# Neighbourhood attention, two heads at a time, on alternating halves of the matmul array

## The chip, the core and the metric

The kernel runs on one core of a Trainium2 chip. TensorE (PE) multiplies a stationary operand of at most 128 rows by 128 columns, loaded by a separate instruction (PEld), with a moving one and writes PSUM, which has eight banks of 128 partitions by 512 float32. VectorE (DVE), ScalarE (ACT) and GpSimd (POOL) work beside it, SyncE (SP) issues most DMA transfers. Each engine works through its own queue in order. The metric is device time of one execution: 2326.95 us, median of 3 runs (2325.53 to 2333.34).

## What is computed

Two transformer blocks follow each other, on 512 positions and 1024 features, in float32. The first has differential attention, gated linear attention and a large expert layer; the second has a Fourier mix, a convolution, a neighbourhood attention and an MLP. The change lies in the neighbourhood attention of the second block. There 8 heads of 64 features look from each of 8 x 64 grid positions at 8 rows by 16 columns around them, and at 256 context positions:

```python
s_loc = jnp.einsum("brqhd,brkhd->bhrqk", qg, kg) * scale + bias[None]
s_ctx = jnp.einsum("brqhd,bchd->bhrqc", qg, k_ctx) * scale
p = jax.nn.softmax(jnp.concatenate([s_loc, s_ctx], axis=-1), axis=-1)
o = (jnp.einsum("bhrqk,brkhd->brqhd", p[..., :n_loc], vg)
     + jnp.einsum("bhrqc,bchd->brqhd", p[..., n_loc:], v_ctx))
```

The output goes, with those of the Fourier mix and the convolution, through the projection `w_out` and is added to the stream `h`.

## The kernel before

Positions are stored column by column of the grid, so a block `b` of 128 queries is 16 grid columns, and its keys are 256 neighbouring positions from `KSTART[b]` on, with the columns out of reach masked by the bias. With 4 blocks and 8 heads there are 32 items; item `i` is head `i // 4`, block `i % 4`. Features of two heads share a tile of 128 partitions: head `h` lies in partitions `64 * (h % 2)` on of `ql`, `kl` (local keys) and `ks` (context keys).

One item runs in three stages, which `pipe` sets against each other by 0, 2 and 3 items:
- `na_scores`: the bias is fetched; scores of 128 queries against 256 local and 256 context keys go into one PSUM bank. Each of the two products is three matmuls (`mm3`, L221 to L223), since operands are split into a high and a low part. DVE adds the bias to the local half and takes the negative row maximum, ACT takes the exponential with a row sum, DVE the reciprocal and the scaling.
- `na_turn`: four transposes through PE into another bank, copied to `npt` by ACT.
- `na_out`: four matmuls (float32, two records each in the trace) of 64 value columns with `npt`, into partitions 0 to 63 of a bank that four blocks of a head fill; behind the fourth, `split` writes the high part (ACT) and the low part (DVE) into the mix tiles.

A fourth entry, `aside`, advances the convolution (`conv`) and the Fourier mix (`fourier`) by one piece per item, in the order of the list `side`. All PSUM tiles of the stage are `psB`, eight of one bank each. The order of instructions on each engine is the scheduler's, which works from the order of the code and the tiles' readiness; what it made of it is shown below.

Ahead of the stage, the values are projected, DVE ends the convolution's taps and then scales `h1` eight times (L1588). Behind it comes `w_out`: for each of 8 output tiles `wsplit` fetches 128 x 1024 weights, ACT and POOL split them, and PE runs 24 matmuls into `pa` (lines L221 to L223 again). The first weights of the MLP are fetched and prepared by `prep` in the same place.

One other place matters below: `da_scores`, in the first block. Its heads have two parts of 64 features each, in partitions 0 to 63 and 64 to 127; for each 128 queries it issues two matmuls of the lower part, into one PSUM tile of two banks, and then two of the upper part, into another:

```python
for c in range(2):
    p = psA()
    for hf in range(2):
        cs = slice(64 * c, 64 * c + 64)
        PE.matmul(p[:, hf, :264], qz[cs, h, nt * 128:nt * 128 + 128], kr[cs, h, hf * 264:hf * 264 + 264], ...)   # L757
```

Of the kernel before, what the change touches and what calls it, by code (L numbers as in the profile page):

```python
# [8 lines left out]
F32 = mybir.dt.float32  # L9
# [5 lines left out]
AF = mybir.ActivationFunctionType  # L15
OP = mybir.AluOpType
AX = mybir.AxisListType
# [5 lines left out]
N = 512  # L23
# [165 lines left out]
def program(tc, a, dbg=None):  # L189
    dbg = dbg or {}  # L190
    nc = tc.nc
# [28 lines left out]
    def mm3(out, lhs, rhs, first, last):  # L220
        PE.matmul(out, lhs[0], rhs[0], start=first, stop=False)  # L221
        PE.matmul(out, lhs[0], rhs[1], start=False, stop=False)  # L222
        PE.matmul(out, lhs[1], rhs[0], start=False, stop=last)  # L223

    def pipe(n, *stages):

        for i in range(n + max(g for _, g in stages)):
            for f, g in stages:
                if 0 <= i - g < n:
                    f(i - g)  # L230

    def split(hi, lo, raw, eng=V):
        S.copy(hi, raw)  # L233
        eng.tensor_sub(lo, raw, hi.bitcast(F32))  # L234
# [38 lines left out]
    def psB():  # L273
        return ps.tile([128, 512], F32, name="psB", bufs=4)
# [1333 lines left out]
    with ExitStack() as es:  # L1608
# [68 lines left out]
                yield  # L1677


        st_ = {}  # L1680

        def na_scores(i):
            h, b = divmod(i, 4)
            k0 = KSTART[b] * 8
            bias = nbp.tile([128, 256], F32, name="bias", bufs=4)
            nc.sync.dma_start(bias, a['nab'][b, h])
            p = psB()
            o = 64 * (h % 2)
            q = [t[o:o + 64, h // 2, b * 128:b * 128 + 128] for t in ql]
            mm3(p[:, 0:256], q, [t[o:o + 64, h // 2, k0:k0 + 256] for t in kl], True, True)  # L1690
            mm3(p[:, 256:512], q, [t[o:o + 64, h // 2] for t in ks], True, True)
            V.tensor_add(p[:, 0:256], p[:, 0:256], bias)
            z = np_.tile([128, 2], F32, name="nz", bufs=5)
            V.reduce_max(z[:, 0:1], p, AX.X, negate=True)
            e = np_.tile([128, N], F32, name="ne", bufs=3)
            S.activation(e, p, AF.Exp, bias=z[:, 0:1], accum_out=z[:, 1:2])
            V.reciprocal(z[:, 1:2], z[:, 1:2])
            V.tensor_scalar(e, e, z[:, 1:2], None, op0=OP.mult)
            st_[i] = e

        def na_turn(i):
            e = st_.pop(i)
            p = psB()
            for k in range(4):
                PE.transpose(p[:, k * 128:k * 128 + 128], e[:, k * 128:k * 128 + 128], ident)
            pt = np_.tile([128, 4, 128], F32, name="npt", bufs=3)
            S.copy(pt, p.rearrange("p (a b) -> p a b", a=4))
            st_['t', i] = pt

        def na_out(i):  # L1710
            h, b = divmod(i, 4)
            k0 = KSTART[b] * 8
            pt = st_.pop(('t', i))
            if b == 0:
                st_['o'] = psB()
            po_ = st_['o']
            for k in range(4):
                vv = vl[:, k0 // 64 + 2 * k] if k < 2 else vc[:, k - 2]
                PE.matmul(po_[:64, b * 128:b * 128 + 128], vv[:, h * 64:h * 64 + 64], pt[:, k], start=k == 0, stop=k == 3)
            if b == 3:  # L1720
                o = (h % 2) * 64
                split(mix[0][o:o + 64, 4 + h // 2], mix[1][o:o + 64, 4 + h // 2], po_[:64])

        def aside(i):
            for g in side[i:i + 1]:
                next(g, None)

        cg, fg = conv(), fourier()
        side = [cg] * 3 + [fg, cg, fg, cg] + [fg, cg] * 3 + [fg] * 8
        pipe(32, (aside, 0), (na_scores, 0), (na_turn, 2), (na_out, 3))  # L1730

    if 'mix2' in dbg:
        with tc.tile_pool(name="dbgp", bufs=1, reuse_waits="tile") as dbp:
# [184 lines left out]
```

## Time and profile before

| | |
|---|---|
| median of 3 runs | 2326.95 us |
| profiled execution | 2328.06 us |
| its span | 2326.3 us |
| mean granted TensorE clock | 0.986 of full speed |
| PE busy | 2237.2 us, 96% |
| DVE busy | 1720.4 us, 74% |
| ACT busy | 1005.9 us, 43% |
| POOL busy | 620.7 us, 27% |

Shares are means over a program of many stages; the attention of the second block takes about a twentieth of the span, from about 1788 to 1903 us. An instruction's time in the trace includes its way through the engine: matmuls that follow each other overlap, so their cost is read from start to start, not from their durations. The granted clock is 1.00 at 2.4 GHz and 0.50 at 1.2 GHz; a window's value is a mean.

### The profile page before, as it was taken

The page shows a single profiled execution, that of the slowest core. Times are in us where ns is not written, and L with a number is a line of the kernel's source. Part 1 is how long each engine was busy: PE and PEld are TensorE (multiplying, and loading weights), DVE is VectorE, ACT ScalarE, POOL GpSimd, SP SyncE. Part 2 cuts the span into 40 slices and gives each one's busy share as a digit, 9 for nine tenths or more (in the row PEclk, how much of TensorE's full clock was granted, in tenths as well). Part 3 has the DMA queues.
Part 4 walks back from the last instruction along what each step waited for, and adds up shares of the span by engine and source line. Part 5 has one row for each costly group of instructions (what it writes and reads, how often), then busy time and mean ns, then how long its engine had stood idle before and what let it go on. Part 6 is the DMA issues. An engine that isn't in the chain of part 4 may idle for free.

```text
span 2326.3 us, 31023 instructions
## 1 busy us (share of the span) xinstructions
PE 2237.2 (96%) x11457; PEld 1884.1 (81%) x11457; DVE 1720.4 (74%) x3188; ACT 1005.9 (43%) x1439; POOL 620.7 (27%) x418
## 2 busy tenths in 40 slices
PE   7999898999999989999999999999998999999997
PEld 6777456898889978889999999999776777888885
DVE  8998776799999778877777887878669566433434
ACT  5337774433378833333333333333344644322322
POOL 2113212344320122223343444444362022000001
PEclk9999999999999999999999999999999999999998
DMA  7760014433266899999899999999322221422320
GB/s 249 253 234 10 1 61 145 172 124 118 85 238 261 301 371 337 335 335 319 309 332 323 313 327 318 322 325 316 130 91 73 73 75 64 126 92 82 118 82 37
DMA packets 158153, 458.02 MB, mean 197 GB/s; under 512 B 15249, under 2 KB 61969, under 8 KB 155697
## 3 DMA queue, kind: packets, MB, share of 16 engines
q1 hardware_dynamic: 120800, 319.57, 39.7%
q0 software_dynamic: 37200, 136.46, 16.9%
q8 instruction: 90, 1.47, 0.3%
q14 instruction: 63, 0.51, 0.1%
HBM read 419.80 MB, written 36.18 MB: 196 GB/s over the span
## 4 chain that ended last, share of the span: by engine, by line
PE 77%; DVE 14%; ACT 3%; DMA 3%; issue 2%; POOL 1%; DVEq 0%; SPq 0%; POOLq 0%; ACTq 0%
PE pu L221 8%; PE po L222 7%; PE po L221 7%; PE po L223 7%; PE pu L222 7%; PE pu L223 7%; DVE ac L1516 3%; PE pm L222 2%; PE pm L223 2%; PE pm L221 2%; PE pa L221 2%; PE pa L222 2%; PE pa L223 2%; PE pq L1187 2%; DVE aw L322 2%
## 5 line engine op out<-in xcount | busy, mean ns | idle before, releaser
L221 PE MATMUL pu<-hn,uhi 128*128 128x384 f32 x1024 | 356.9, 349 | 1.4 <-ACT uhi L233 1.4
L223 PE MATMUL pu<-hn,ulo 128*128 128x384 f32 x1024 | 347.3, 339 | 5.4 <-DVE ulo L234 3.6
L222 PE MATMUL pu<-hn,uhi 128*128 128x384 f32 x1024 | 347.4, 339 | 0.0
L221 PE MATMUL po<-vhi,ch 128*128 128x512 f32 x768 | 301.1, 392 | 2.5 <-ACT ch L1308 2.5
L222 PE MATMUL po<-vlo,ch 128*128 128x512 f32 x768 | 301.2, 392 | 0.3 <-DVE vlo L1309 0.3
L223 PE MATMUL po<-vhi,cl 128*128 128x512 f32 x768 | 299.0, 390 | 0.0
L1200 POOL DMA_INDIRECT gr<-in_u,idx x128 | 144.9, 1132 | 445.9 <-DVE aact L1205 414.6
L233 ACT CAST whi<-wraw 128x1024 fp32r<-128x1024 f32 x104 | 108.8, 1049 | 321.2 <-PE pm L222 128.7
L1297 ACT CAST vhi<-vraw 128x1024 fp32r<-128x1024 f32 x128 | 134.8, 1053 | 250.7 <-PE po L223 129.0
L234 POOL TENSOR_TENSOR wlo<-wraw,whi 128x1024 fp32r<-128x1024 f32 x52 | 130.8, 2521 | 382.7 <-ACT whi L233 329.2
L233 ACT CAST uhi<-uraw 128x1024 fp32r<-128x1024 f32 x105 | 110.1, 1048 | 268.9 <-PE pu L222 241.3
L1200 POOL DMA_INDIRECT gr<-in_v,idx x128 | 156.7, 1224 | 226.7 <-DVE acc L1214 189.1
L223 PEld LDWEIGHTS pu<-hn,ulo 128*128 128x128 f32 x1024 | 192.6, 188 | 6.4 <-DVE ulo L234 3.9
L221 PEld LDWEIGHTS pu<-hn,uhi 128*128 128x128 f32 x1024 | 193.0, 188 | 5.4 <-ACT uhi L233 1.9
L222 PEld LDWEIGHTS pu<-hn,uhi 128*128 128x128 f32 x1024 | 193.2, 189 | 3.5
L1309 DVE TENSOR_TENSOR vlo<-vraw,vhi 128x1024 fp32r<-128x1024 f32 x128 | 156.3, 1221 | 47.4 <-ACT vhi L1297 47.4
L234 DVE TENSOR_TENSOR wlo<-wraw,whi 128x1024 fp32r<-128x1024 f32 x52 | 63.5, 1222 | 157.6 <-ACT whi L233 157.4
L223 PEld LDWEIGHTS po<-vhi,cl 128*128 128x128 f32 x768 | 144.6, 188 | 31.7 <-DVE cl L1310 0.3
L221 PEld LDWEIGHTS po<-vhi,ch 128*128 128x128 f32 x768 | 144.6, 188 | 31.3 <-ACT ch L1308 2.9
L222 PEld LDWEIGHTS po<-vlo,ch 128*128 128x128 f32 x768 | 144.4, 188 | 27.9 <-DVE vlo L1309 0.7
L1214 DVE SCALAR_TENSOR_TENSOR acc<-gr,aact,acc 128x1024 f32<-128x1024 f32 x126 | 154.4, 1277 | 0.0
L1205 DVE CUSTOM_DVE_ANT_0 gr<-gr,hnat 128x1024 f32<-128x1024 f32 x128 | 152.5, 1218 | 0.0
(584 smaller groups left out, 5066.8 us busy)
## 6 DMA issues: line engine op xcount, KB each, us to landing
uraw<-in_ut SPq DMA_DIRECT2D x129, 512.0 KB, 4.9
vraw<-in_v SPq DMA_DIRECT2D x128, 512.0 KB, 5.5
aw<-in_ada SPq DMA_DIRECT2D x48, 512.0 KB, 5.0
gt<-gd SPq DMA_DIRECT2D x42, 480.0 KB, 7.4
wraw<-in_m SPq DMA_DIRECT2D x32, 512.0 KB, 3.7
xraw<-in_m SPq DMA_DIRECT2D x32, 512.0 KB, 4.3
gd<-gs SPq DMA_DIRECT2D x6, 2048.0 KB, 10.1
sd<-ge SPq DMA_DIRECT2D x56, 192.0 KB, 2.3
```

The costliest lines, as they stand in the source:

```text
L221: PE.matmul(out, lhs[0], rhs[0], start=first, stop=False)
L222: PE.matmul(out, lhs[0], rhs[1], start=False, stop=False)
L223: PE.matmul(out, lhs[1], rhs[0], start=False, stop=last)
L233: S.copy(hi, raw)
L234: eng.tensor_sub(lo, raw, hi.bitcast(F32))
L322: V.tensor_tensor_reduce(out=t, in0=w, in1=sil[:, q], scale=1.0, scalar=0.0, op0=OP.mult, op1=OP.add, accum_out=o)
L1200: G.indirect_dma_start(r, None, src, bass.IndirectOffsetOnAxis(ap=idx[:, j:j + 1], axis=0))
L1205: V.tensor_tensor_reduce(out=r, in0=r, in1=hnat, scale=1.0, scalar=0.0, op0=OP.mult, op1=OP.add, accum_out=aact[:, j:j + 1])
L1214: V.scalar_tensor_tensor(A, r, aact[:, j:j + 1], A, op0=OP.mult, op1=OP.add)
L1297: S.copy(wh, raw)
L1309: V.tensor_sub(wl, raw, wh.bitcast(F32))
L1516: V.scalar_tensor_tensor(ac[:, t], cv[:, t, j:j + N], w, ac[:, t], op0=OP.mult, op1=OP.add)
```

## The change

The 32 items become 16, each a pair of heads (`hp`) and a block. `na_scores` takes two banks and issues the same matmul for the head in partitions 0 to 63 and for the one in 64 to 127 in turn; `na_turn` transposes both heads; `na_out` alternates between output partitions 0 to 63 and 64 to 127 of one bank, and one `split` of 128 partitions follows four blocks. The small tiles move into a pool of their own (`nae`), with 6 buffers for the exponentials (three pairs) and 4 for the transposed ones (two pairs). The list `side` is shorter, and `aside` now stands behind the scores.

```diff
@@ -1677,57 +1677,68 @@
                 yield
 
 
+
         st_ = {}
+        nep = es.enter_context(tc.tile_pool(name="nae", bufs=1, reuse_waits="tile"))
+        HALVES = (slice(0, 64), slice(64, 128))
 
         def na_scores(i):
-            h, b = divmod(i, 4)
+            hp, b = divmod(i, 4)
             k0 = KSTART[b] * 8
-            bias = nbp.tile([128, 256], F32, name="bias", bufs=4)
-            nc.sync.dma_start(bias, a['nab'][b, h])
-            p = psB()
-            o = 64 * (h % 2)
-            q = [t[o:o + 64, h // 2, b * 128:b * 128 + 128] for t in ql]
-            mm3(p[:, 0:256], q, [t[o:o + 64, h // 2, k0:k0 + 256] for t in kl], True, True)
-            mm3(p[:, 256:512], q, [t[o:o + 64, h // 2] for t in ks], True, True)
-            V.tensor_add(p[:, 0:256], p[:, 0:256], bias)
-            z = np_.tile([128, 2], F32, name="nz", bufs=5)
-            V.reduce_max(z[:, 0:1], p, AX.X, negate=True)
-            e = np_.tile([128, N], F32, name="ne", bufs=3)
-            S.activation(e, p, AF.Exp, bias=z[:, 0:1], accum_out=z[:, 1:2])
-            V.reciprocal(z[:, 1:2], z[:, 1:2])
-            V.tensor_scalar(e, e, z[:, 1:2], None, op0=OP.mult)
-            st_[i] = e
+            bias, pp, es_ = [], [psB(), psB()], []
+            for h in range(2):
+                bias.append(nbp.tile([128, 256], F32, name="bias", bufs=4))
+                nc.sync.dma_start(bias[h], a['nab'][b, 2 * hp + h])
+            for keys, at, sl in ((kl, 0, slice(k0, k0 + 256)), (ks, 256, slice(0, 256))):
+                for t, (x, y) in enumerate(((0, 0), (0, 1), (1, 0))):
+                    for p, o in zip(pp, HALVES):
+                        PE.matmul(p[:, at:at + 256], ql[x][o, hp, b * 128:b * 128 + 128], keys[y][o, hp, sl], start=t == 0,
+                                  stop=t == 2)
+            for p, bt in zip(pp, bias):
+                V.tensor_add(p[:, 0:256], p[:, 0:256], bt)
+                z = nep.tile([128, 2], F32, name="nz", bufs=6)
+                V.reduce_max(z[:, 0:1], p, AX.X, negate=True)
+                e = nep.tile([128, N], F32, name="ne", bufs=6)
+                S.activation(e, p, AF.Exp, bias=z[:, 0:1], accum_out=z[:, 1:2])
+                es_.append((e, z))
+            for e, z in es_:
+                V.reciprocal(z[:, 1:2], z[:, 1:2])
+                V.tensor_scalar(e, e, z[:, 1:2], None, op0=OP.mult)
+            st_[i] = es_
 
         def na_turn(i):
-            e = st_.pop(i)
-            p = psB()
-            for k in range(4):
-                PE.transpose(p[:, k * 128:k * 128 + 128], e[:, k * 128:k * 128 + 128], ident)
-            pt = np_.tile([128, 4, 128], F32, name="npt", bufs=3)
-            S.copy(pt, p.rearrange("p (a b) -> p a b", a=4))
-            st_['t', i] = pt
+            pts = []
+            for e, _ in st_.pop(i):
+                p = psB()
+                for k in range(4):
+                    PE.transpose(p[:, k * 128:k * 128 + 128], e[:, k * 128:k * 128 + 128], ident)
+                pt = nep.tile([128, 4, 128], F32, name="npt", bufs=4)
+                S.copy(pt, p.rearrange("p (a b) -> p a b", a=4))
+                pts.append(pt)
+            st_['t', i] = pts
 
         def na_out(i):
-            h, b = divmod(i, 4)
+            hp, b = divmod(i, 4)
             k0 = KSTART[b] * 8
-            pt = st_.pop(('t', i))
+            pts = st_.pop(('t', i))
             if b == 0:
                 st_['o'] = psB()
             po_ = st_['o']
             for k in range(4):
                 vv = vl[:, k0 // 64 + 2 * k] if k < 2 else vc[:, k - 2]
-                PE.matmul(po_[:64, b * 128:b * 128 + 128], vv[:, h * 64:h * 64 + 64], pt[:, k], start=k == 0, stop=k == 3)
+                for h, o in enumerate(HALVES):
+                    PE.matmul(po_[o, b * 128:b * 128 + 128], vv[:, (2 * hp + h) * 64:(2 * hp + h) * 64 + 64], pts[h][:, k],
+                              start=k == 0, stop=k == 3)
             if b == 3:
-                o = (h % 2) * 64
-                split(mix[0][o:o + 64, 4 + h // 2], mix[1][o:o + 64, 4 + h // 2], po_[:64])
+                split(mix[0][:, 4 + hp], mix[1][:, 4 + hp], po_)
 
         def aside(i):
             for g in side[i:i + 1]:
                 next(g, None)
 
         cg, fg = conv(), fourier()
-        side = [cg] * 3 + [fg, cg, fg, cg] + [fg, cg] * 3 + [fg] * 8
-        pipe(32, (aside, 0), (na_scores, 0), (na_turn, 2), (na_out, 3))
+        side = [cg, fg, cg, fg, cg, fg, cg, fg, cg, fg, cg] + [fg] * 5
+        pipe(16, (na_scores, 0), (aside, 0), (na_turn, 2), (na_out, 3))
 
     if 'mix2' in dbg:
         with tc.tile_pool(name="dbgp", bufs=1, reuse_waits="tile") as dbp:
```

How it moves instructions. On PE, in the late part of the attention, one item stood like this before (`kl0`, `kl1` are the high and low parts of the local keys, `ks` of the context keys, `ql` of the queries; tiles of one name differ by their number):

```order
L221 MATMUL psB_17139<-kl0_15410,ql0_15408 128x256
L222 MATMUL psB_17139<-kl1_15411,ql0_15408 128x256
L223 MATMUL psB_17139<-kl0_15410,ql1_15409 128x256
L221 MATMUL psB_17139<-ks0_15412,ql0_15408 128x256
L222 MATMUL psB_17139<-ks1_15413,ql0_15408 128x256
L223 MATMUL psB_17139<-ks0_15412,ql1_15409 128x256
L1705 MATMUL psB_17153<-ident_58,ne_17092 128x128 x4
L1719 MATMUL psB_17132<-npt_17130,vl_15414 64x128 x2
L1719 MATMUL psB_17132<-npt_17130,vc_15420 64x128 x2
```

Now the two banks of a pair alternate, and so do the two heads' `npt` in the outputs (the last four of the scores, the transposes and the first half of the outputs):

```order
L1695 MATMUL psB_17158<-ks1_15413,ql0_15408 128x256
L1695 MATMUL psB_17159<-ks1_15413,ql0_15408 128x256
L1695 MATMUL psB_17158<-ks0_15412,ql1_15409 128x256
L1695 MATMUL psB_17159<-ks0_15412,ql1_15409 128x256
L1714 MATMUL psB_17190<-ident_58,ne_17069 128x128 x4
L1714 MATMUL psB_17197<-ident_58,ne_17074 128x128 x4
L1730 MATMUL psB_17204<-npt_17139,vl_15414 64x128
L1730 MATMUL psB_17204<-npt_17146,vl_15414 64x128
L1730 MATMUL psB_17204<-npt_17139,vl_15414 64x128
L1730 MATMUL psB_17204<-npt_17146,vl_15414 64x128
```

So between two changes from scores to transposes there stand twelve score matmuls where there were six, eight transposes and eight output matmuls.

On DVE, in the same part, the reciprocal and scaling of an item (L1697, L1698) stood among the bias addition and maximum (L1692, L1694) of the next:

```order
L1692 TENSOR_TENSOR psB_16806<-psB_16806,bias_16804 128x256
L1698 TENSOR_SCALAR ne_16788<-ne_16788,nz_16786 128x512
L1694 TENSOR_REDUCE nz_16814<-psB_16806 128x1
L1692 TENSOR_TENSOR psB_16833<-psB_16833,bias_16831 128x256
L1697 RECIPROCAL nz_16814<-nz_16814 128x1
L1694 TENSOR_REDUCE nz_16841<-psB_16833 128x1
L1698 TENSOR_SCALAR ne_16816<-ne_16816,nz_16814 128x512
L1697 RECIPROCAL nz_16841<-nz_16841 128x1
```

Now, in most pairs, addition (L1698), maximum (L1700), reciprocal (L1705) and scaling (L1706) of the same two heads follow each other:

```order
L1698 TENSOR_TENSOR psB_16812<-psB_16812,bias_16814 128x256
L1698 TENSOR_TENSOR psB_16813<-psB_16813,bias_16816 128x256
L1700 TENSOR_REDUCE nz_16831<-psB_16812 128x1
L1700 TENSOR_REDUCE nz_16836<-psB_16813 128x1
L1705 RECIPROCAL nz_16831<-nz_16831 128x1
L1706 TENSOR_SCALAR ne_16833<-ne_16833,nz_16831 128x512
L1705 RECIPROCAL nz_16836<-nz_16836 128x1
L1706 TENSOR_SCALAR ne_16838<-ne_16838,nz_16836 128x512
L234 TENSOR_TENSOR mx1_16285<-psB_16844,mx0_16284 128x512
```

The reciprocal waits for ACT's exponential of its own head. Work of another item no longer stands between a pair's maxima and its reciprocals; in a few pairs, three of them near the end, the next pair's additions stand between its two reciprocals.

At the start of the stage, PE had the convolution's mean (L1623), one item's scores, and the convolution's second product (L1633):

```order
L1598 MATMUL psB<-ident,sg 128x128 x8
L1623 MATMUL psB<-ac,ones 128x512 x2
L221 MATMUL psB<-kl_15410,ql_15408 128x256
L222 MATMUL psB<-kl_15411,ql_15408 128x256
L223 MATMUL psB<-kl_15410,ql_15409 128x256
L221 MATMUL psB<-ks_15412,ql_15408 128x256
L222 MATMUL psB<-ks_15413,ql_15408 128x256
L223 MATMUL psB<-ks_15412,ql_15409 128x256
L1633 MATMUL psB<-csq,ones 128x512 x2
```

Now a pair's scores stand ahead of the mean, and behind it come the second pair's and the Fourier mix's first products:

```order
L1623 MATMUL psB<-ac,ones 128x512 x2
L1695 MATMUL psB<-kl_15410,ql_15408 128x256 x2
L1695 MATMUL psB<-kl_15411,ql_15408 128x256 x2
L1695 MATMUL psB<-kl_15410,ql_15409 128x256 x2
L1695 MATMUL psB<-ks_15412,ql_15408 128x256 x2
L1695 MATMUL psB<-ks_15413,ql_15408 128x256 x2
L1695 MATMUL psB<-ks_15412,ql_15409 128x256 x2
L1657 MATMUL psB<-dft,ul 128x256 x8
```

The third pair's scores follow, and only then the convolution's second product.

## Rows read from the trace of the kernel before

**Rows 1.** the page, part 1: engine, busy us, share of the span, instructions

```profile
span 2326.3 us, 31023 instructions
PE 2237.2 (96%) x11457; PEld 1884.1 (81%) x11457; DVE 1720.4 (74%) x3188; ACT 1005.9 (43%) x1439; POOL 620.7 (27%) x418
```

**Rows 2.** the timeline, the stage's ends: start us, us, engine, line, operation, tiles, shapes, count

```profile
1788.27 5.39 DVE L1588 SCALAR_TENSOR_TENSOR h<-h,cols,rsy 128x512 f32<-128x512 f32 x8
...
1893.81 13.43 SPq L1756 DMA_DIRECT2D wraw<-in_m  x3
...
1897.56 2.13 DVE L1698 TENSOR_SCALAR ne<-ne,nz 128x512 f32<-128x512 f32 x1
...
1902.65 0.79 PE L221 MATMUL pa<-mx,whi 128*128 128x512 f32 x1
```

**Rows 3.** busy windows: length, PE, PEld, DVE, ACT, POOL (instructions), PEclk, DMA share, GB/s

```profile
1790.00:1795.00 5.00, 0.93 (x7) 0.73 (x7) 5.00 (x9) 0.71 (x2) 0.00 (x0) 1.00 0.03 11
1795.00:1800.00 5.00, 5.00 (x16) 2.80 (x16) 1.32 (x3) 4.48 (x6) 0.00 (x0) 0.66 0.11 26
...
1870.00:1880.00 10.00, 10.00 (x74) 8.11 (x73) 6.95 (x18) 5.85 (x13) 0.00 (x0) 1.00 0.20 55
```

**Rows 4.** the timeline, PE, one head in the late part of the attention

```profile
1870.22 0.38 PE L221 MATMUL psB<-kl,ql 64*128 64x256 f32 x1
...
1871.13 0.66 PE L1705 MATMUL psB<-ident,ne 128*128 128x128 f32 x4
1871.71 0.65 PE L1719 MATMUL psB<-npt,vl 128*64 128x128 f32 x4
...
1872.73 0.39 PE L221 MATMUL psB<-kl,ql 64*128 64x256 f32 x1
```

**Rows 5.** the timeline, scores of the first block's attention: both halves, one half, weight loads

```profile
193.84 1.17 PE L757 MATMUL psA<-kr,qz 64*128 64x264 f32 x8
...
272.84 1.15 PE L757 MATMUL psA<-kr,qz 64*128 64x264 f32 x4
...
193.84 0.20 PEld L757 LDWEIGHTS psA<-kr,qz 64*128 64x128 f32 x2
```

**Rows 6.** the timeline, DVE and ACT, the softmax of one head

```profile
1825.68 0.43 DVE L1692 TENSOR_TENSOR psB<-psB,bias 128x256 f32<-128x256 f32 x1 [2.73 <-PE psB L223]
...
1826.15 0.69 DVE L1694 TENSOR_REDUCE nz<-psB 128x1 f32<-128x512 f32 x1
...
1826.87 0.69 ACT L1696 ACTIVATE ne<-psB,nz 128x512 f32<-128x512 f32 x1
...
1827.68 0.16 DVE L1697 RECIPROCAL nz<-nz 128x1 f32<-128x1 f32 x1 [0.84 <-ACT ne L1696]
...
1827.88 0.49 DVE L1698 TENSOR_SCALAR ne<-ne,nz 128x512 f32<-128x512 f32 x1
```

**Rows 7.** the timeline, DVE and ACT, instructions that follow each other at once

```profile
1800.70 0.41 DVE L1692 TENSOR_TENSOR psB<-psB,bias 128x256 f32<-128x256 f32 x1
...
1801.02 0.47 DVE L1698 TENSOR_SCALAR ne<-ne,nz 128x512 f32<-128x512 f32 x1
1801.41 0.68 DVE L1694 TENSOR_REDUCE nz<-psB 128x1 f32<-128x512 f32 x1
...
1802.08 0.69 ACT L1696 ACTIVATE ne<-psB,nz 128x512 f32<-128x512 f32 x1
...
1802.76 0.68 ACT L1696 ACTIVATE ne<-psB,nz 128x512 f32<-128x512 f32 x1
```

**Rows 8.** instruction groups by line, 1790 to 1905: busy us, mean ns, idle before

```profile
L1707 ACT COPY npt<-psB 128x512 f32<-128x512 f32 x32 | 18.7, 585 | 23.1 <-PE psB L1705 23.0
...
L234 DVE TENSOR_TENSOR mx<-psB,mx 64x512 fp32r<-64x512 f32 (+1 forms) x10 | 6.8, 682 | 6.7 <-ACT mx L233 6.7
...
L1639 ACT ACT_TABLE_LOAD x2 | 2.6, 1283 | 0.0
```

**Rows 9.** busy windows, in the first block's attention, columns as in rows 3

```profile
235.00:240.00 5.00, 3.74 (x20) 2.68 (x19) 3.62 (x7) 5.00 (x14) 1.26 (x2) 1.00 0.00 0
```

## Prediction

> **What bounds the kernel now.** I read the page's part 1, then the busy windows around the attention, then the timeline of one head there, and last the rows of DVE and ACT between. The program is bound by TensorE: PE is busy for 96% of a span of 2326.3 us [rows 1], so time saved on another engine pays only where PE waits. The stage that changes begins where DVE ends the rescaling of `h1`, at 1788.27 + 5.39 = 1793.66, and ends with the first matmul of the output projection at 1902.65 [rows 2]: 109.0 us, 4.7% of the span. Two things fill it. From about 1805 on PE never rests: in 1870 to 1880 it is busy for all 10 us, DVE for 6.95, ACT for 5.85 [rows 3]. At the start PE is busy for 0.93 us of 5, a hole of 4.07, and then runs 5 us at a mean granted clock of 0.66 (1.2 GHz for most of it) [rows 3].
>
> One head and block costs PE 1872.73 - 1870.22 = 2.51 us in the late, undisturbed part: scores 0.91, four transposes 0.58, eight output matmul records 1.02 (a float32 matmul leaves two records) [rows 4]. 32 of them are 80.3 us. So the side work on PE (convolution and Fourier products) with all other waits is at most 109.0 - 80.3 - 4.1 = 24.6.
>
> **Removed and added on PE: scores.** A head's scores use 64 of the array's 128 rows, and the kernel before gives all of a head's matmuls the same half. Whether two halves run beside each other is shown in the first block's attention, whose scores have 64 rows as well: with one half alone four records take 1.15 us; with four on the lower half, then four on the upper, eight take 1.17, and two weight loads begin within the same 0.20 us [rows 5]. So eight cost what four cost, and I price twelve score matmuls of a pair like six: 0.91 us instead of 1.82.
>
> **Outputs.** They alternate between column halves, which this trace nowhere does: 16 records of a pair take between 1.02 (full overlap) and 2.04 (none). I take 1.02, since the nearest rows, those on row halves, show full overlap of matmuls and of loads.
> The Trainium skill, "TensorE: Matmul & The Clock Gate", Measured speedup vs the span model, gives 2.38 times for three column tiles; an estimate from it is 1.6 for two, so 1.28 us, and the sum below would stay, since PE isn't its bound. No run so far shows it.
>
> **Transposes** stay at eight per pair, 1.16. PE's step is then 0.91 + 1.16 + 1.02 = 3.09 us per pair against 5.02; 16 steps and the side work are 49.4 + 24.6 = 74.0, or 16 x 4.11 + 24.6 = 90.4 if column halves queue. None of DVE's and ACT's work on the scores goes away, so they are late next.
>
> **DVE and ACT.** In the new order DVE does a step as add, add, reduce, reduce, and then the reciprocals and scalings of the same two heads, which wait for both exponentials on ACT. The chain of one pair, by rows of single heads: first add 0.32 (to the next instruction), second add to its reduce 0.47, reduce to exponential 0.72, first to second exponential 0.68, exponential to reciprocal 0.81, reciprocal to scaling 0.20, scaling to the next instruction 0.39 [rows 6, 7]. Sum 3.59 us per pair, 57.4 for 16. Its bound from below is DVE's work alone: the 6.95 us busy in 1870 to 1880 hold one subtraction of 0.68 and 10/2.51 heads, so 1.57 a head, 3.15 a pair, 50.4 for 16 [rows 3, 8]. A few steps of the new order do mix pairs, so the truth lies between; I take 57.4, since most steps stand in series.
>
> What comes on top:
> - ACT's table loads. Per step ACT has 3.59 less two exponentials (0.68) and two copies (0.585), so 1.06 us free. Three times a side function needs two loads of 1.28 and an activation as long as an exponential, 0.69, 3.3 each [rows 6, 8]: 3 x (3.3 - 1.06) = 6.7. The first exponential's load adds 1.28. Together 8.0. ACT's other side work, 18 copies and casts of 0.59 and two weight casts of about twice that (twice the columns), is 13.0 and fits into the 17.0 free in 16 steps.
> - DVE's side work: 15 instructions like the subtraction of 0.68 and four like the add of 0.43, 11.9 us [rows 6, 8]. DVE stands still 3.59 - 3.15 = 0.44 a step, 7.0 in all; the order is fixed, so I let half of it take side work: 8.4.
> - The end: from the last scaling's end, 1897.56 + 2.13 = 1899.69, to 1902.65 were 2.96 us [rows 2]; a pair has four more transposes, 0.58: 3.5.
> - Waits that no row shows, for PSUM banks above all: eight banks; two pairs of scores, one pair of transposes and one output tile take seven, a side product the eighth. Lower end nothing; upper end the scores of the next pair in series with DVE each time, 0.91 x 16 = 14.6. I take 3, near the lower end, because seven fit.
>
> Sum: 57.4 + 8.0 + 8.4 + 3.5 + 3 = 80.3 us from 1793.66, against 109.0: 28.7 gained. PE needs 74.0 and may start before: two pairs' scores and sixteen Fourier records now stand ahead of the convolution's second product, where the hole of 4.07 was.
>
> **What moves along.** The biases are the same 32 transfers; two are freed per step and four buffered. The weights of the projection are split by ACT two steps before the end. SP issues the first MLP load at 1893.81, when the last scores are done, 8.8 us before the projection [rows 2]; now that distance is about 3.6 + 3.5 = 7.1, so POOL's work on it may come up to 2 us late for PE; I put it at 0 and keep 2 for the range. Everything behind is as long as before and moves forward as a block.
>
> The profiled execution took 2328.06 us, 1.1 above the median of the three timed (2326.95). 2328.1 - 28.7 = 2299.4, less 1.1: **2298 us**.
>
> **Rivals.**
> 1. *Column halves queue.* PE bounds: from about 1788.3, 90.4 + 3.5 end at 1882.2, 20.5 earlier than 1902.65: 2306. For it: no row shows columns side by side. Against: rows of the array do.
> 2. *Hand-offs.* The next pair's scores wait for banks that ACT hasn't emptied; the upper end of the waits, 14.6 for 3: a gain of 17, 2310, and some us more where a Fourier step takes two banks. The Trainium skill, "TensorEngine Tiling (Array Packing)", PSUM Bottleneck, warns of this: tiling speeds up TensorE but not the emptying of PSUM. The trace agrees as far as DVE and ACT are already busy for 70% and 59% of 1870 to 1880 [rows 3].
> 3. *The halves don't overlap at all* (the change doesn't do what it says): 80.3 + 24.6 from 1788.3, plus 3.5, ends at 1896.7; only the hole goes, 6 us: 2321. Against it stand the rows of the first attention [rows 5].
> 4. *Slower: the clock falls.* PE, now waiting for DVE in each step, is granted 1.2 GHz through the stage, and its 74.0 us become 148: the end at 1788.3 + 148 + 3.5 = 1939.8 is 37 later, 2364. It decides once PE is the bound at that clock, that is when over half the stage runs so (74.0 + half of 74.0 passes 109). For it: after the hole of 4.07 us the mean was 0.66. Against: in 235 to 240 PE is busy for 3.74 of 5 us and the clock stays 1.00 [rows 9], and a step with 3.09 of some 4.5 us busy is more like that.
>
> **How the numbers follow.** The forecast has 0.61, its own range 2288 to 2306 (DVE's bound from below takes 7 off, hand-offs and the late MLP load put up to 8 on). Rival 1 has 0.17, rival 2 0.13, rival 3 0.05, rival 4 0.04. The range 2286 to 2314 leaves out rivals 3 and 4, a third of rival 2 and the forecast's faster tail, under 0.2. A difference under 0.3%, 7 us, is about what a measurement of this kernel can't tell from none; rival 3 is within it. So faster 0.91, same 0.05, slower 0.04.
>
> **What would show it.** In the profile after: score matmuls in pairs, twelve in about 0.9 us; sixteen output records in about 1.0 (1.3 still fits, 2.0 is rival 1); steps of 3.5 to 4.5 us with DVE waiting for ACT's exponentials and PE idle for about a us in each; clock 1.00; the first projection matmul about 80 us behind the rescaling's end. A step over 4.6 us with DVE waiting for PE's scores would be rival 2, a mean clock under 0.8 over the stage rival 4. The forecast is wrong if the first projection matmul comes less than 15 us earlier than before.

## The result, and the profile after

The changed kernel takes **2298.09 us** (median of 4 runs, 2296.13 to 2300.76), the kernel before 2328.18 us (median of 4, 2325.53 to 2333.34): a ratio of 0.9866, 95% interval 0.9853 to 0.9879. The profiled execution took 2299.26 us.

The page of the changed kernel, its span and part 1, against [rows 1]:

```profile
span 2297.4 us, 31031 instructions
...
PE 2208.4 (96%) x11457; PEld 1862.9 (81%) x11457; DVE 1715.4 (75%) x3184; ACT 999.7 (44%) x1435; POOL 622.6 (27%) x418
```

The timeline of the changed kernel at the stage's ends, against [rows 2]:

```profile
1791.79 5.39 DVE L1588 SCALAR_TENSOR_TENSOR h<-h,cols,rsy 128x512 f32<-128x512 f32 x8
...
1860.26 17.26 SPq L1767 DMA_DIRECT2D wraw<-in_m  x3
...
1873.04 0.64 PE L221 MATMUL pa<-mx,whi 128*128 128x512 f32 x1
```

The stage runs from 1791.79 + 5.39 = 1797.18 to 1873.04: 75.9 us against 109.0, so 33.1 less. The spans differ by only 28.9, because the stage began 3.5 us later in this execution, and what follows it took 424.4 us against 423.7. The code ahead is the same; over the profiled kernels of this case DVE's L1588 starts anywhere from 1784.4 to 1794.2, so those 3.5 us are within the spread between executions.

The busy windows over the stage, first of the kernel before, then of the changed one (length, PE, PEld, DVE, ACT, POOL with their instructions, PEclk, DMA share, GB/s):

```profile
1793.66:1902.65 108.99, 103.59 (x630) 76.92 (x631) 66.04 (x150) 67.03 (x129) 6.78 (x3) 0.96 0.23 68
```

```profile
1797.18:1873.04 75.86, 68.98 (x606) 51.47 (x604) 61.04 (x146) 60.68 (x125) 6.78 (x3) 0.96 0.32 98
...
1810.00:1820.00 10.00, 7.95 (x60) 6.84 (x60) 8.96 (x20) 9.66 (x15) 0.00 (x0) 0.83 0.24 72
...
1830.00:1840.00 10.00, 10.00 (x83) 6.86 (x84) 8.68 (x23) 7.06 (x17) 0.00 (x0) 1.00 0.14 42
1840.00:1850.00 10.00, 10.00 (x92) 7.04 (x94) 8.32 (x20) 8.00 (x18) 0.00 (x0) 1.00 0.27 72
1850.00:1860.00 10.00, 10.00 (x128) 8.40 (x124) 8.58 (x21) 9.30 (x22) 4.88 (x2) 1.00 0.82 270
1860.00:1873.00 13.00, 9.55 (x92) 7.46 (x88) 8.22 (x19) 6.88 (x16) 1.90 (x1) 0.88 0.36 123
```

PE is busy for 34.6 us less in this window and stands still for 6.9 us instead of 5.4: 34.6 - 1.5 = 33.1. The window's start hides a shift. While DVE runs L1588, just ahead of it, PE was busy for half of the time before and is busy for all of it now:

```profile
1788.27:1793.66 5.39, 2.64 (x11) 1.19 (x9) 5.39 (x9) 0.59 (x1) 0.00 (x0) 1.00 0.34 129
```

```profile
1791.79:1797.18 5.39, 5.39 (x37) 3.70 (x37) 5.39 (x9) 0.59 (x1) 0.00 (x0) 1.00 0.34 129
```

With that stretch counted in, PE is busy for 74.4 us instead of 106.2, 31.9 less, and stands still for 6.9 instead of 8.2.

DVE and ACT are busy for 80% of the stage now, where it was 61%. In the middle, from 1812.12 to 1860.79, PE still never waits. One step there, the timeline of PE, against the head in [rows 4]:

```profile
1850.36 0.62 PE L1695 MATMUL psB<-kl,ql 64*128 64x256 f32 x6
1850.82 0.52 PE L1695 MATMUL psB<-ks,ql 64*128 64x256 f32 x6
1851.27 1.09 PE L1714 MATMUL psB<-ident,ne 128*128 128x128 f32 x8
1852.29 0.66 PE L1730 MATMUL psB<-npt,vl 128*64 128x128 f32 x8
1852.78 0.61 PE L1730 MATMUL psB<-npt,vc 128*64 128x128 f32 x8
1853.32 0.62 PE L1695 MATMUL psB<-kl,ql 64*128 64x256 f32 x6
```

Twelve scores take 0.91 us, as six did; sixteen output records 1.03, as eight did (1.02); eight transposes 1.02 instead of twice 0.58. A pair costs 2.96 us instead of 5.02. Over 16 pairs that is 14.6 from the rows, 16.2 from the columns and 2.2 from the transposes: 33.0, against the 31.9 by which PE's busy time fell. The overlap accounts for the gain to about 1 us.

PE's waits in the stage sum to 6.9 us. They stand at both ends; four of the seven, in order of time:

```profile
1800.29 0.62 PE L1695 MATMUL psB<-kl,ql 64*128 64x256 f32 x5 [0.80 <-DVE ac L1625]
...
1812.12 1.01 PE L1695 MATMUL psB<-kl,ql 64*128 64x256 f32 x5 [2.05 <-DVE crb L252]
...
1864.37 0.63 PE L1714 MATMUL psB<-ident,ne 128*128 128x128 f32 x4 [0.49 <-DVE ne L1706]
...
1868.38 0.63 PE L1714 MATMUL psB<-ident,ne 128*128 128x128 f32 x4 [2.14 <-DVE nz L1705]
```

The second is a wait for a PSUM bank: the scores take the bank that DVE's L252 reads last for the convolution. The last two wait for the softmax; ahead of the 2.14 a scaling took 1.3 us longer than elsewhere, beside POOL (last section).

### The profile page after: what moved, and what is told of

Its sections match the earlier page's. It is cut to its first block, busy times and chain, and to the rows that moved or that the text cites. A ratio compares the mean times of both kernels' runs of the same rounds, so it can differ in the third digit from the quotient of the medians.

```text
span 2297.4 us, 31031 instructions
## 1 busy us (share of the span) xinstructions
PE 2208.4 (96%) x11457; PEld 1862.9 (81%) x11457; DVE 1715.4 (75%) x3184; ACT 999.7 (44%) x1435; POOL 622.6 (27%) x418
## 4 chain that ended last, share of the span: by engine, by line
PE 74%; DVE 7%; ACT 2%; issue 2%; DMA 1%; POOL 1%; DVEq 0%; SPq 0%; POOLq 0%; ACTq 0%
PE pu L221 8%; PE pu L223 8%; PE pu L222 8%; PE po L222 7%; PE po L221 7%; PE po L223 7%; DVE ac L1516 3%; PE pa L221 2%; PE pa L222 2%; PE pa L223 2%; PE pm L222 2%; PE pm L223 2%; PE pm L221 2%; PE pq L1187 2%; PE pq L223 1%
## 5 line engine op out<-in xcount | busy, mean ns | idle before, releaser
L234 POOL TENSOR_TENSOR wlo<-wraw,whi 128x1024 fp32r<-128x1024 f32 x52 | 132.1, 2546 | 381.3 <-ACT whi L233 220.3
L234 DVE TENSOR_TENSOR wlo<-wraw,whi 128x1024 fp32r<-128x1024 f32 x52 | 63.6, 1223 | 160.0 <-ACT whi L233 159.9
L221 PEld LDWEIGHTS po<-vhi,ch 128*128 128x128 f32 x768 | 144.4, 188 | 31.9 <-ACT ch L1308 3.3
```

## The experiments

Two theories were open. By the first, TensorE bounds the stage after the change too. By the second, that of the prediction, the chain through VectorE and ScalarE bounds it. In the table the stage is measured as above, from DVE's L1588 to the first matmul of the projection; "behind" is from there to the span's end. Kernels that ran together shared their runs of before, so ratios compare best; their intervals are 0.0013 to 0.0018 either way, 3 to 4 us (0.0010 for the fifth row).

| kernel | median us | ratio to before | stage us | PE busy, idle | behind us |
|---|---|---|---|---|---|
| changed kernel | 2298.1 | 0.9866 | 75.9 | 69.0, 6.9 | 424.4 |
| one column half | 2304.0 | 0.9904 | 83.4 | 80.1, 3.4 | 424.6 |
| scores by head | 2296.5 | 0.9871 | 73.9 | 68.1, 5.8 | 424.1 |
| outputs by head | 2297.5 | 0.9872 | 76.1 | 73.4, 2.7 | 424.6 |
| before, scores first | 2329.0 | 1.0003 | 106.2 | 100.8, 5.4 | 424.9 |
| side product first | 2297.5 | 0.9864 | 76.5 | 70.8, 5.7 | 424.4 |
| no scaling | 2292.9 | 0.9853 | 69.5 | 67.2, 2.3 | 424.3 |
| half of the outputs | 2292.5 | 0.9832 | 72.8 | 65.4, 7.4 | 424.1 |
| end filled | 2302.9 | 0.9892 | 72.1 | 66.9, 5.2 | 432.8 |
| end filled, root earlier | 2303.5 | 0.9895 | 72.7 | 67.4, 5.4 | 431.6 |
| side spread | 2297.9 | 0.9867 | 73.8 | 68.9, 4.8 | 427.0 |
| spread, scaling on ACT | 2297.0 | 0.9861 | 75.7 | 68.5, 7.2 | 424.9 |
| scaling on ACT | 2297.7 | 0.9858 | 74.9 | 69.2, 5.7 | 424.9 |

**One column half.** The outputs of both heads go to the lower column half:

```
-                for h, o in enumerate(HALVES):
-                    PE.matmul(po_[o, b * 128:b * 128 + 128], ...
+            for h in range(2):
+                c = h * 256 + b % 2 * 128
...
+                    PE.matmul(po_[:64, c:c + 128], ...
```

Expected:

> The output matmuls of both heads of a pair go to the same half of the array's columns (partitions 0 to 63 of a bank that two blocks share); scores, transposes and the order of the steps stay. If TensorE bounds the stage, a pair's 16 records cost 2.04 us instead of the 1.03 seen, at 16 steps: +16.2 us on 2298, so 2314. If the chain on VectorE and ScalarE bounds it, as the prediction has it, only what passes the chain counts: TensorE's 90.4 us against the chain's 80.3, of which an early start gives some back: +8, so 2306. If column halves never ran beside each other, no change: 2298.

The timeline of PE in this kernel, one pair's output matmuls and the scores behind them:

```profile
1854.81 0.65 PE L1731 MATMUL psB<-npt,vl 128*64 128x128 f32 x4
1855.30 0.60 PE L1731 MATMUL psB<-npt,vc 128*64 128x128 f32 x4
1855.74 0.60 PE L1731 MATMUL psB<-npt,vl 128*64 128x128 f32 x4
1856.17 0.60 PE L1731 MATMUL psB<-npt,vc 128*64 128x128 f32 x4
1856.70 0.62 PE L1695 MATMUL psB<-kl,ql 64*128 64x256 f32 x6
```

Sixteen records take 1.89 us here, against 1.03 on two halves: the column halves do run beside each other. But 16 x 0.86 = 13.8 us of added matmul time made the kernel 5.9 us slower (8.8 by the ratios) and the stage 7.6 us longer. PE's busy time grew by 11.1 us and its waits fell by 3.5, from 6.9 to 3.4: with a step of 3.82 us (1852.88 to 1856.70) the waits at the end are gone, and so is the one for a bank. The other 2.7 of the 13.8 stay open. The edit also splits the outputs by head, behind every second block; that gives DVE 12 and ACT 11 more instructions, so the slowdown need not be PE's alone. That part of the price went into waits speaks for the second theory; the fullness of PE in the middle spoke for the first.

**The order of issue.** Two runs take the alternation away and leave the halves: in the one the scores (t, then head) are issued by head, in the other the outputs (k, then head).

```
-                for t, (x, y) in enumerate(((0, 0), (0, 1), (1, 0))):
-                    for p, o in zip(pp, HALVES):
+                for p, o in zip(pp, HALVES):
+                    for t, (x, y) in enumerate(((0, 0), (0, 1), (1, 0))):
```

> The twelve score matmuls of a pair are issued as six of the one head and then six of the other, on the same halves of the rows as before. If issue order does not matter for the overlap (as in the first block's attention, where four on one half follow four on the other), within 2 us of 2298. If only neighbours on different halves overlap, twelve cost 1.82 us instead of 0.91 and with TensorE as the bound 16 steps add 14.6: 2312; with the chain on VectorE and ScalarE as the bound, +6 at most: 2304.

> The sixteen output records of a pair are issued as eight of the one column half and then eight of the other. If issue order does not matter, within 2 us of 2298, and 16 records still take about 1.03 us in the trace. If only neighbours on different column halves overlap, 2.04 us, and with TensorE as the bound +16.2: 2314; with the chain on VectorE and ScalarE as the bound +8: 2306.

The first edit is milder than its expectation says: the loop over the keys stays outside, so it issues three of one head, then three of the other, twice. Twelve scores still take 0.92 us (1853.96 to 1854.88 in its trace). The outputs, eight records of one half and then eight of the other, overlap in part. PE's timeline in that kernel, most single records left out:

```profile
1852.47 0.65 PE L1730 MATMUL psB<-npt,vl 128*64 128x128 f32 x4
1852.95 0.27 PE L1730 MATMUL psB<-npt,vc 128*64 128x128 f32 x1
1852.96 0.32 PE L1730 MATMUL psB<-npt,vl 128*64 128x128 f32 x1
1853.07 0.27 PE L1730 MATMUL psB<-npt,vc 128*64 128x128 f32 x1
...
1853.45 0.60 PE L1730 MATMUL psB<-npt,vc 128*64 128x128 f32 x4
1853.98 0.62 PE L1695 MATMUL psB<-kl,ql 64*128 64x256 f32 x6
```

The second head's first record starts beside the first head's fifth, at 1852.96, and the sixteen take 1.51 us: a quarter of them alone at the front, a quarter alone at the end. So issue order matters for long runs on one half and not for three. Yet the kernel's time is the same, as the second theory has it: PE is busy for 4.4 us more and idle for 4.1 us less. (By the rows of one pair it would be busy for 16 x 0.48 = 7.7 more; the mean granted clock was 0.98 in this stage, against 0.96.)

**Order of the parts in a step.** The two kernels swap `na_scores` and `aside` in the call of `pipe`.

> The kernel before, with the one order taken over from the change: in each step the scores come ahead of the side product. One head at a time, one half of the rows, as before. If the gain comes from the matmuls that run beside each other alone, 2327 with no more than 2 us of difference. If part of it is the order (scores fill the hole of about 4 us at the start of the stage, and the side product delays the next scores less), 2 to 5 us less: 2323.

> The changed kernel with the old order in a step: the side product ahead of the scores. If order is worth nothing, 2298. If scores ahead of the convolution's first product are what filled the hole at the start, the hole comes back in part: 2300 to 2303. If the side product ahead helps (the convolution's chain through VectorE and ScalarE starts one score group, 0.9 us, earlier), up to 2 us less.

Neither order moved the time (1.0003, interval 0.9993 to 1.0012; and 0.9864 beside 0.9866). In the trace of the first the stage is 2.8 us shorter, and 1.2 of it comes back behind; the timing does not show the rest. The gain is not from the order. Two parts of the change have no run of their own. The overlap of the row halves rests on the rows alone, twelve scores in 0.91 us where six took that before. The larger buffers and the pairing on DVE could have helped only where PE waited before, at the stage's ends.

**Lightening one side.** The first of these two leaves out DVE's L1706; the second issues the output matmuls for `k` in `range(2)`.

> Leaves out the scaling of the exponentials by the reciprocal of their sum (32 instructions of VectorE, 0.39 us each from one to the next); TensorE's work is the same. If the chain on VectorE and ScalarE bounds the stage, the chain of a pair loses 0.20 + 0.39 + part of the wait for the second exponential, at least 0.6 x 16 = 9.6 us: 2288. If TensorE bounds it, only the end after the last exponentials (where the transposes wait for the scaling) gets shorter, by 1 to 3 us: 2296.

> Leaves out half of the output matmuls of each pair (the keys of the second 256 columns, 8 of 16 records); VectorE and ScalarE do what they did. TensorE's step falls from 2.96 to 2.45 us. If TensorE were the bound with room below it, 16 x 0.51 = 8.2 us less: 2290. If the chain on VectorE and ScalarE is the next bound right behind it, as the waits at the end suggest, nearly all of it turns into waits: 2296 to 2298.

Each median lies between its two expectations. Without the scaling the medians differ by 5.2 us, by the ratios only by 3, and the intervals of the two ratios overlap: the times alone do not settle it. In the trace the stage is 6.4 us shorter with PE's work unchanged. 4.6 of it are PE's waits, which fall from 6.9 to 2.3: those at the end sum to 0.50 instead of 3.44, and the one for a bank is gone (0.27 for a copy by ACT came in). The other 1.8 are PE's busy time, at a mean granted clock of 0.98 instead of 0.96. The scalings that POOL stretches at the end (last section) are left out with the others, so this run does not tell the length of the chain from POOL's part in it.

With half of the outputs PE has 7.2 us less to do by its rows (a pair's eight records take 0.58 us, 1851.80 to 1852.38 in its trace, instead of 1.03). The stage loses 3.0, PE is busy for 3.6 less, and it waits for 7.4 us. This execution is the slowest of its five, and the 12 us behind its wait for the bank (1811.67 to 1823.67) ran at a mean granted clock of 0.59. The medians differ by 5.6, the ratios by 8 us, clear of the intervals, so the timing says more than this one trace and its size stays open. Both sides bind, each in its part of the stage. The timeline of DVE in the changed kernel shows where:

```profile
1805.42 1.28 DVE L1700 TENSOR_REDUCE nz<-psB 128x1 f32<-128x512 f32 x2
...
1808.94 1.28 DVE L1700 TENSOR_REDUCE nz<-psB 128x1 f32<-128x512 f32 x2
...
1834.13 1.28 DVE L1700 TENSOR_REDUCE nz<-psB 128x1 f32<-128x512 f32 x2
...
1839.23 1.28 DVE L1700 TENSOR_REDUCE nz<-psB 128x1 f32<-128x512 f32 x2
...
1843.35 1.28 DVE L1700 TENSOR_REDUCE nz<-psB 128x1 f32<-128x512 f32 x2
...
1857.27 1.27 DVE L1700 TENSOR_REDUCE nz<-psB 128x1 f32<-128x512 f32 x2
...
1860.90 1.27 DVE L1700 TENSOR_REDUCE nz<-psB 128x1 f32<-128x512 f32 x2
...
1864.74 1.28 DVE L1700 TENSOR_REDUCE nz<-psB 128x1 f32<-128x512 f32 x2
```

Near the start, with no other work of DVE between them, a pair's reductions come 3.52 us after the last pair's: the chain in series. In the middle they come 5.10 and 4.12 us apart, 4.61 on average, at about the pace of PE's steps with a side product (4.72 us, twelve matmuls to twelve matmuls from 1840.92 to 1845.64). In the last steps, with no side product left, they come 3.63 and 3.84 us apart, while PE's steps take 2.96. PE runs ahead by 0.7 us a step or more and pays it back in the waits at the end. Not all of that is the chain: the 3.63 holds a scaling that POOL stretches by 0.39 (last section), the 3.84 a subtraction for the mix (L234) of 0.60. Without them both would be 3.24, an estimate.

**Filling the end.** If the waits at the end are such a debt, work moved there should fill them. The last Fourier product and the last convolution product go into the last two steps; a second kernel also computes the convolution's root one step earlier.

```
+        def late(i):
+            if i >= 14:
+                next((fg, cg)[i - 14])
...
-        pipe(16, (na_scores, 0), (aside, 0), (na_turn, 2), (na_out, 3))
+        pipe(16, (na_scores, 0), (aside, 0), (late, 2), (na_turn, 2), (na_out, 3))
```

> The last side product of the Fourier part and the last of the convolution (four matmul records, 1.8 us each) move from the steps in which TensorE has no need of them into the last two steps, ahead of the transposes that waited 0.33, 0.48, 0.49 and 2.14 us for VectorE. If TensorE bounds the middle of the stage and the chain on VectorE and ScalarE only its end, the two products fill 3.4 us of waits and spare the stretch at a granted clock of 0.66 behind them (some 1.5 us): 3 to 5 us less, 2294. If the chain bounds the whole stage, the products only move: within 1 us of 2298. If their splits come too late for the projection, 1 to 2 us more.

> As the run with the filled end, and the convolution's reciprocal root comes one step earlier, so that its PSUM bank is free before the scores that waited 2.05 us for it. If that wait and the stretch at a granted clock of 0.69 behind it cost TensorE, another 2 to 3.5 us less: 2291. If VectorE and ScalarE are the bound there, the wait only moves: as the run with the filled end, 2294.

A miss with a lesson. The waits at the end did go (POOL's multiplications left the stage as well), and the stage is 3.8 us shorter; but the kernel is about 5 us slower, for behind the stage it takes 8.5 us more. The execution traced is the fastest of the four, 2296.6 us; it began the stage 7.4 us earlier than that of the changed kernel. The timeline of PE and of SP's queue in the kernel with the filled end:

```profile
1846.36 11.74 SPq L238 DMA_DIRECT2D wraw<-in_wout  x3
...
1861.87 0.50 PE L221 MATMUL pa<-mx,whi 128*128 128x512 f32 x1 [1.62 <-ACT whi L233]
...
1864.31 0.80 PE L223 MATMUL pa<-mx,wlo 128*128 128x512 f32 x1 [1.70 <-POOL wlo L234]
...
1885.77 2.08 PE L862 MATMUL pa<-nsq,ones 128*128 128x512 f32 x2 [3.88 <-DVE nsq L861]
```

And its waits, of SP's queue:

```profile
SPq L238 <- PE psB L1644: 10.1, 1, 10.1
```

A load of the projection's weights waits 10.1 us for the convolution's last product (L1644). In the code the two pools, `conv` and `wo2`, lie on the same side of SBUF, so the loads wait until the side products have read their tiles. Behind the stage PE then waits 1.70 us for POOL's part of the weights and 3.88 instead of 1.26 at L862, and the first 39 us ran at a mean granted clock of 0.87, in the changed kernel at 1.00. Side products that end early do more than give PE work: they free the memory for what comes next. The earlier root did not help either; it left a wait of 1.51 us for L252 in front of another matmul.

**Spreading the side work, and the last scaling on ACT.** Three runs, of two edits and both together:

```
-        side = [cg, fg, cg, fg, cg, fg, cg, fg, cg, fg, cg] + [fg] * 5
+        no = iter(())
+        side = [cg, fg, cg, fg, cg, fg, cg, fg, cg, no, fg, cg, no, fg]
```

```
-                V.tensor_scalar(e, e, z[:, 1:2], None, op0=OP.mult)
+                if i == 15:
+                    S.activation(e, e, AF.Copy, scale=z[:, 1:2])
+                else:
+                    V.tensor_scalar(e, e, z[:, 1:2], None, op0=OP.mult)
```

> The last three side products move from the steps 9, 10 and 11 (counted from 0) to 10, 11 and 13, so that fewer of the last steps are without one; the memory that they use comes free four steps before the stage's end, not at it. If the waits at the end are a debt that VectorE and ScalarE run up in the steps without side work (3.6 us a step against TensorE's 2.96), two such steps fewer take 2 x 0.65 and the waits that follow off, 1 to 3 us less than 2298, and the projection does not wait for its weights. If the weights of the projection are late again, as with the filled end, 2300 or more.

> The changed kernel with the two scalings of the last pair on ScalarE, nothing else. The last wait of TensorE, 2.14 us, falls to about 1 if GpSimd's multiplication is what stretched VectorE's scaling: 2297. If it was something else, the same as the changed kernel, 2298; a wait for ScalarE instead, up to 1 us more.

> As the run with the side products spread, and the two scalings of the last pair go from VectorE to ScalarE (which idles then), because VectorE's last scaling took 1.76 us beside a multiplication of GpSimd, against 0.47 elsewhere. If the two engines disturb each other there, the last transposes start about 1 us earlier: 1 to 1.5 us less than with the spread alone. If not, no change.

None differs from the changed kernel by more than the measurement can tell. Spreading took 2.1 us off the stage and gave 2.7 back behind it, where PE now waits 0.51 us for POOL's part of the projection's weights. With the scaling on ACT the last wait fell from 2.14 to 1.30, but another grew: the timeline of POOL and of DVE in that kernel,

```profile
1858.91 2.35 POOL L234 TENSOR_TENSOR wlo<-wraw,whi 128x1024 fp32r<-128x1024 f32 x1 [0.93 <-ACT whi L233]
```

```profile
1858.91 2.63 DVE L1709 TENSOR_SCALAR ne<-ne,nz 128x512 f32<-128x512 f32 x1
```

Here a scaling of an earlier pair met a multiplication of POOL, took 2.63 us and made PE wait 1.96. No version tried that does the whole computation beats the changed kernel by more than the measurement can tell.

## Why the prediction was right, and where it was not

The time came out at 2298.1 for a forecast of 2298; that closeness is partly luck. The stage came out 4.4 us shorter than forecast, and the profiled execution gave 3.5 of that back by beginning it later, within the spread between executions. Against its own runs of before the kernel gained 30.1 us by the medians and 31.2 by the ratio, where the forecast had 29.

- **Rows and columns overlap: right.** Forecast 0.91 and 1.02 us for a pair, measured 0.91 and 1.03. The sum was said to stand even at 1.28 for the outputs, because PE would not be its bound. The run with the outputs by head has 1.51 and the same time.
- **The estimate from three column tiles: low.** From the 2.38 times of the Trainium skill, "TensorE: Matmul & The Clock Gate", Measured speedup vs the span model, the prediction had estimated 1.6 for two column halves. They gave 1.89 / 1.03 = 1.8.
- **PE's step: nearly.** 2.96 instead of 3.09, as eight transposes in one run take 1.02, not 1.16. The 74.0 us that PE needs "and may start before" came out at 74.4: 69.0 in the stage and 5.4 ahead of it, the convolution's mean included.
- **The failed step: "57.4 + 8.0 + 8.4 + 3.5 + 3 = 80.3".** Measured 75.9. The chain itself was about right, 3.59 forecast, 3.52 in series. What failed is taking it for the bound of all 16 steps and adding ACT's table loads, DVE's side work and the bank waits to it in series. From 1812.12 to 1860.79, 48.7 of the 75.9 us, PE never waits: there its steps, 2.96 us and longer with a side product, set the pace, and the added terms run beside them. From the first pair's reductions (1797.76) to the last's (1864.74) 15 steps take 67.0 us, 4.47 each, where the forecast has (80.3 - 3.5) / 16 = 4.80. How much of each term was hidden no run separates.
- **"PE idle for about a us in each step": wrong.** PE is full from 1830 to 1860 and stands still at the two ends.
- **The hole at the start: filled, with a new one behind it.** Scores and Fourier records fill it as forecast; of its 4.07 us 0.80 and 0.56 are left, for the convolution's DVE and ACT work. Then come 2.05 for a bank, with a mean granted clock of 0.83 in 1810 to 1820. The idle time within the stage looks no smaller than before only because 2.8 of the 4.07 lay ahead of 1793.66. The 3 us put down for bank waits met this one of 2.05, not a little in each step.
- **The end: 3.5 forecast, 4.2 measured** (the second scaling ends at 1868.83, the projection starts at 1873.04). What the sum did not see stands in front of it: the first of the two scalings took 1.76 us instead of 0.47, for the reason in the last section. The 2.13 in [rows 2] was that already: the scaling ended at 1899.69 there, 0.29 behind this multiplication of POOL in the kernel before.

```profile
1897.51 1.89 POOL L1758 TENSOR_TENSOR wb<-wraw,mod 128x1024 f32<-128x1024 f32 x1 [38.58 <-DMA wraw<-in_m]
```

- **The MLP load: right.** Behind the stage 0.7 us more than before, within the 0 to 2.
- **The rivals.** *Column halves queue* was priced at 2306; the run that forces them to queue took 2304.0, with some more work on DVE and ACT. *Hand-offs* occurred once, for a bank that the convolution held, not in each step. *No overlap* is excluded by the 0.91 and the 1.03. *The clock* fell only at both ends, behind PE's two longest waits: to 0.52 from 1812.12 to 1815.50 and to 0.67 from 1868.38 to 1873.04; its mean over the stage is 0.96, as before. So such a wait costs more than its length: behind the 2.05, eleven scores and eight transposes took 3.37 us, where twelve and eight take 0.91 + 1.02 at 1.00, about 1.4 us more.

## What to carry to other kernels

When two bounds of a stage are close, add each side work to the bound that it lengthens, not to their sum: the steps with PE side work were PE's, the steps without were the softmax's, and taking work from either side alone returned only part of it. Look for the waits at both ends of a stage that is full in its middle; they are the other bound's bill, unless an instruction there is longer than its like elsewhere: POOL's part showed only so. Before moving work later, look at whose memory it holds: here it delayed the next weights by more than it saved.

## What the runs showed of the hardware

**A scaling on DVE stands until POOL's operation ends.** DVE's TENSOR_SCALAR of 128x512 from SBUF takes 0.47 to 0.49 us alone. In the changed kernel, timelines of POOL and of DVE:

```profile
1866.05 1.90 POOL L1769 TENSOR_TENSOR wb<-wraw,mod 128x1024 f32<-128x1024 f32 x1 [6.48 <-DMA wraw<-in_m]
```

```profile
1866.47 1.76 DVE L1706 TENSOR_SCALAR ne<-ne,nz 128x512 f32<-128x512 f32 x1
```

It ends at 1868.23, 0.28 us after POOL's end at 1867.95, though a profile counts all of it as busy. With half of the outputs the rows are

```profile
1857.85 2.37 POOL L234 TENSOR_TENSOR wlo<-wraw,whi 128x1024 fp32r<-128x1024 f32 x1 [1.91 <-ACT whi L233]
```

```profile
1859.12 1.38 DVE L1706 TENSOR_SCALAR ne<-ne,nz 128x512 f32<-128x512 f32 x1
...
1860.50 0.66 DVE L1700 TENSOR_REDUCE nz<-psB 128x1 f32<-128x512 f32 x1
```

again 0.28 after POOL's end (1860.22), and in the kernel with the scaling on ACT 1861.54 against 1861.26, also 0.28. In the last steps of the changed kernel it happens twice more, once in

```profile
1857.07 2.50 POOL L234 TENSOR_TENSOR wlo<-wraw,whi 128x1024 fp32r<-128x1024 f32 x1 [1.12 <-ACT whi L233]
```

```profile
1858.99 0.86 DVE L1706 TENSOR_SCALAR ne<-ne,nz 128x512 f32<-128x512 f32 x1
```

Over the profiles of this case 22 scalings of the stage begin with 0.3 us or more of a POOL multiplication still to run, and all 22 end 0.28 or 0.29 us behind it. One that begins first is not stretched: 0.47 us from 1856.88, 0.19 ahead of the POOL row above. The Trainium skill, "SBUF — State Buffer", Who interferes with whom, says that DVE in a two-port mode and GpSimd share a port pair, and that the later one is blocked for the whole instruction. The traces agree in all 22; whether the scaling runs in a two-port mode no row shows.

**How far apart two halves may be issued.** Three and three (scores, 0.92 us for twelve) and four and four [rows 5] overlap fully; eight and eight records overlap from the fifth on (1.51 us, between 1.03 and 1.89). In that kernel's program all eight records of the first head stand ahead of the second's, yet the second's first starts at 1852.96, ahead of the first's sixth at 1853.07. So the queue "in order" of the section on the chip does not hold for PE's matmuls on different halves.
